# Masked attention in a six-layer decoder: the two terms of the scores issued term by term for a group of heads instead of head by head

## The chip, the cores and the metric

The kernel runs on one core of one Trainium2 chip. The metric is the device time of one execution in microseconds (us); for the kernel before it is the median of three runs. A core has TensorE (PE in the profile; PEld is its weight load), VectorE (DVE), ScalarE (ACT), GpSimd (POOL) and SyncE (SP), which issues the transfers.

## The reference, cut to what matters

Two stacks of layers follow one another on a sequence of 256 tokens of width 1024: four layers (windowed attention, a gated linear recurrence, MLA attention, windowed attention again, each with a cross attention to a memory and a gated feed-forward part), then two layers (attention with forget gates, here called fox, and dilated attention, each with memory heads and a feed-forward part). All is computed in float32. In two of them a score is the sum of two terms. The MLA layer has eight heads, and a causal mask:

```
sc = (einsum('bqhd,bkhd->bhqk', qn_b, k_nope)
      + einsum('bqhd,bkd->bhqk', qr_b, k_rope)) * scale
sc = where(key_pos[None, :] <= q_pos[:, None], sc, NEG)
p = softmax(sc)
```

Here `qn_b` and `k_nope` have 128 features for a head, the rotated parts `qr_b` and `k_rope` 64, and `k_rope` is shared by the heads. The fox layer has twelve heads of 64 features, and `c` is the running sum of the logarithm of the forget gates:

```
sc = einsum('bhqd,bhkd->bhqk', qi, k) * scale
sc = sc + ci[..., :, None] - c[..., None, :]
sc = where(kpos[None, :] <= qpos[:, None], sc, NEG_2)
p = softmax(sc)
```

Every other attention (windowed, dilated, cross and memory heads) has a single feature product in its score.

## The kernel before, in words

The tokens lie in two tiles of 128 (t = 0 and 1). Projections are built from `mm3` (L87 to L89): both factors are split into a rounded part and a rest in the format fp32r, and three products are accumulated. A weight is loaded by SyncE, rounded by ScalarE (`hi`, L76) and its rest taken by VectorE (`lo`, L81).

All attentions go through `attend` (called from `cross`, `swa`, `mla` and `mix`), once for each query tile, with 128 or 256 keys for tile 0 and 1 where the attention is causal. It works through groups of heads (eight heads at 128 keys, four at 256) in three steps: `scores` makes the scores of a group in two PSUM banks and their softmax, `turn` transposes the probabilities on TensorE (L334), `values` multiplies them by the values (L354). Scores of one group are issued ahead of the turn and the values of earlier ones. Heads alternate between the two banks: even heads go to bank 0, odd heads to bank 1.

Where a mask is given, `pre` writes it into both banks first, by products with a unit matrix (L291); fox adds the first half of the gate term there. Then `score(h)` gives the terms of head h, a list of pairs of a stationary and a moving operand, which are accumulated onto the open bank (L300). Without `pre` (cross attention and memory heads) each head is an accumulation of its own (L298). What `score` returns:

- `mla`: two terms, `(qT, kT)` of 128 rows in plain float32 (in the profile `xh,qT`, as the keys lie in the buffer `xh`), and `(qT, krT)` of 64 rows in plain float32, rows 0 to 63 for even and 64 to 127 for odd heads;
- fox (`mix(0)`): two terms, `(sel, cT)` of 128 rows in fp32r (in the profile `cT,sel`), and `(qT, kT)` of 64 rows in plain float32 (`kv,qT`), again the lower rows for even and the upper for odd heads;
- windowed (`swa`) and dilated (`mix(1)`) attention: one term of 64 rows in the same manner.

After the scores, VectorE takes the row maxima (L308), ScalarE the exponentials with their sums (L315), VectorE scales them (L321, L324); copies out of PSUM alternate between the two (`evac`, L62 and L64). In `mla` the query blocks of the last head groups are rotated on VectorE (L262 to L265), transposed (L161) and copied out (L64) just ahead of the first scores.

The order on each engine is not that of the source alone: a scheduler of the framework places instructions of neighbouring steps among one another, so that a few `mm3` of the next projection stand between parts of an attention. Each engine then executes its own instructions in that order and waits for the others by semaphores.

Of the kernel before, what the change touches and what calls it, by code (L numbers as in the profile page):

```python
# [34 lines left out]
def model_kernel(ctx: ExitStack, tc: tile.TileContext, A, out):  # L35
    nc = tc.nc
    V, S, G, T = nc.vector, nc.scalar, nc.gpsimd, nc.tensor
# [9 lines left out]
    def bank(tag="r"):  # L47
        return psum.tile([P, 512], F32, tag=tag, name="bank", bufs=4 if tag == "r" else 2)

    def bank_of(t):  # L50
        return bank(f"t{t}")
# [7 lines left out]
    def evac(dst, src):  # L59
        count["ev"] += 1  # L60
        if count["ev"] % 2:
            S.copy(dst, src)  # L62
        else:
            V.tensor_copy(dst, src)  # L64
# [26 lines left out]
    def split(hi, lo, src):  # L91
        S.copy(hi, src)  # L92
        V.tensor_tensor(lo, src, hi, ALU.subtract)

    def tile_cols(t):
        return slice(t * P, (t + 1) * P)
# [182 lines left out]
    def attend(ph, t, heads, d, keys, score, value, scale=1.0, pre=None, sinks=None, base=0, pb=2, tb=4):  # L279
        nk = keys // P  # L280
        size = 2 * (512 // keys)
        oth, otl = cur["o"]

        def scores(h0):
            n = min(size, heads - h0)
            g = n // 2
            banks = [bank()[:, : g * keys].rearrange("p (h n) -> p h n", n=keys) for _ in range(2)]
            if pre is not None:
                for b in range(2):
                    for j, (l, r) in enumerate(pre(slice(h0 + b, h0 + n, 2), g)):  # L290
                        T.matmul(banks[b], l, r, start=(j == 0), stop=False)  # L291
            for i in range(g):
                for b in range(2):
                    terms = score(h0 + 2 * i + b)
                    for j, (l, r) in enumerate(terms):
                        last = j == len(terms) - 1
                        if pre is None:
                            T.matmul(banks[b][:, i], l, r, start=(j == 0), stop=last)  # L298
                        else:
                            T.matmul(banks[b][:, i], l, r, start=False, stop=(last and i == g - 1))  # L300
            nm = sm.tile([P, 8], F32, tag="nm", name="nm")
            den = sm.tile([P, 8], F32, tag="den", name="den")
            pr = ph.tile([P, 2, 512], F32, tag="pr", name="pr", bufs=pb)
            prv = pr[:, :, : g * keys].rearrange("p b (h n) -> p b h n", n=keys)
            rd = sm.tile([P, 8], F32, tag="rd", name="rd")
            for b in range(2):
                c = slice(b * g, b * g + g)
                V.tensor_reduce(nm[:, c], banks[b], AX.X, ALU.max, negate=True)  # L308
                if sinks is not None:
                    V.tensor_tensor(nm[:, c], nm[:, c], sinks[1][:, h0 + b : h0 + n : 2], ALU.min)  # L310
                if scale != 1.0:
                    V.tensor_scalar(nm[:, c], nm[:, c], scale, None, ALU.mult)
                for i in range(g):
                    j = slice(b * g + i, b * g + i + 1)
                    S.activation(prv[:, b, i], banks[b][:, i], AF.Exp, bias=nm[:, j], scale=scale, accum_out=den[:, j])  # L315
                if sinks is not None:
                    es = sm.tile([P, 4], F32, tag="es", name="es")
                    V.tensor_tensor(es[:, :g], nm[:, c], sinks[0][:, h0 + b : h0 + n : 2], ALU.add)
                    S.activation(es[:, :g], es[:, :g], AF.Exp)
                    V.tensor_tensor(den[:, c], den[:, c], es[:, :g], ALU.add)  # L320
                V.reciprocal(rd[:, c], den[:, c])  # L321
                for i in range(g):
                    j = slice(b * g + i, b * g + i + 1)
                    V.tensor_scalar(prv[:, b, i], prv[:, b, i], rd[:, j], None, ALU.mult)  # L324
            return h0, n, prv

        def turn(h0, n, prv):
            pT = {}
            items = [(h, kt) for b in range(2) for h in range(b, n, 2) for kt in range(nk)]
            for o in range(0, len(items), 4):  # L330
                part = items[o : o + 4]
                tp = bank_of(t)
                for j, (h, kt) in enumerate(part):
                    T.transpose(tp[:, tile_cols(j)], prv[:, h % 2, h // 2, tile_cols(kt)], ident)  # L334
                dst = ph.tile([P, 4, P], F32, tag="pT", name="pT", bufs=tb)
                m = len(part)
                evac(dst[:, :m], tp[:, : m * P].rearrange("p (h n) -> p h n", n=P))
                for j, it in enumerate(part):
                    pT[it] = dst[:, j]
            return h0, n, pT  # L340

        def values(h0, n, pT):
            per = max(1, P // d)
            cols = n * d // P
            for c0 in range(0, cols, 4):
                nc_ = min(4, cols - c0)
                po = bank_of(t)
                for c in range(c0, c0 + nc_):
                    for i in range(per):
                        h = (c * P) // d + i  # L350
                        w = min(d, P)
                        off = (c * P) % d if d > P else 0
                        for kt in range(nk):
                            T.matmul(  # L354
                                po[i * w : (i + 1) * w, tile_cols(c - c0)],
                                value(h0 + h, kt)[:, off : off + w],
                                pT[h, kt],
                                start=(kt == 0),
                                stop=(kt == nk - 1),
                            )  # L360
                b0 = base + h0 * d // P + c0
                view = po[:, : nc_ * P].rearrange("p (b n) -> p b n", n=P)
                split(oth[:, b0 : b0 + nc_, tile_cols(t)], otl[:, b0 : b0 + nc_, tile_cols(t)], view)

        todo = list(range(0, heads, size))
        made, turned = [], []
        for i in range(len(todo) + 2):
            if i < len(todo):
                made.append(scores(todo[i]))
            if i >= 2:  # L370
                values(*turned.pop(0))
            if 1 <= i <= len(todo):
                turned.append(turn(*made.pop(0)))
# [415 lines left out]
    def load_norms(l):  # L789
        gb = par.tile([P, 2, D], F32, tag="gb", name="gb", bufs=1)  # L790
        nc.sync.dma_start(gb, A["norms"][l].partition_broadcast(P))
        return gb
# [169 lines left out]
    for i in range(4):  # L962
        kind, j = i % 3, i // 3
# [10 lines left out]
    with phase("g") as ph:  # L974
        g = ph.tile([P, D], F32, tag="g", name="g", bufs=1)
# [6 lines left out]
    g = load_norms(0)  # L982
# [3 lines left out]
    g = load_norms(1)  # L986
# [129 lines left out]
```

## Time and profile before

| what | value |
|---|---|
| runs | 2142.24, 2142.79, 2148.39 us, median 2142.79 us |
| span of the profiled execution | 2141.0 us |
| TensorE busy | 2103.1 us, 98% |
| weight loads (PEld) busy | 1869.3 us, 87% |
| VectorE, ScalarE, GpSimd busy | 1616.3, 1219.2, 84.4 us |
| mean granted clock of TensorE | 0.987 of full speed |
| read from memory | 354.81 MB, 166 GB/s over the span |

The span goes from the first to the last instruction of one profiled execution. TensorE's matmuls are pipelined, so the durations of neighbours overlap and the pace is read from the difference of two start times. A plain float32 product leaves two records in the profile, an fp32r product one. The granted clock is a share of 2.4 GHz: 1.00 is the full 2.4 GHz, 0.50 is 1.2 GHz.

### The profile page before, as it was taken

The page shows a single profiled execution, that of the slowest core. Times are in us where ns is not written, and L with a number is a line of the kernel's source. Part 1 is how long each engine was busy: PE and PEld are TensorE (multiplying, and loading weights), DVE is VectorE, ACT ScalarE, POOL GpSimd, SP SyncE. Part 2 cuts the span into 40 slices and gives each one's busy share as a digit, 9 for nine tenths or more (in the row PEclk, how much of TensorE's full clock was granted, in tenths as well). Part 3 has the DMA queues.
Part 4 walks back from the last instruction along what each step waited for, and adds up shares of the span by engine and source line. Part 5 has one row for each costly group of instructions (what it writes and reads, how often), then busy time and mean ns, then how long its engine had stood idle before and what let it go on. Part 6 is the DMA issues. An engine that isn't in the chain of part 4 may idle for free.

```text
span 2141.0 us, 36194 instructions
## 1 busy us (share of the span) xinstructions
PE 2103.1 (98%) x13528; PEld 1869.3 (87%) x13528; DVE 1616.3 (75%) x3344; ACT 1219.2 (57%) x2654; POOL 84.4 (4%) x77
## 2 busy tenths in 40 slices
PE   8999999999999999999999999999999999999998
PEld 7778999887999986899997789998878999978997
DVE  6877877898777784787788778888458877677775
ACT  5545656585555563555555456564446566456664
POOL 0010000122000001000000100000000000000000
PEclk9999999999999997999999999999999999999999
DMA  8533655526455461556544347654325655524651
GB/s 329 179 109 125 222 186 187 180 93 230 160 196 185 129 208 40 177 187 193 182 159 148 118 147 247 197 178 156 136 79 187 215 181 166 188 92 158 201 184 60
DMA packets 101409, 358.23 MB, mean 167 GB/s; under 512 B 11888, under 2 KB 13552, under 8 KB 99312
## 3 DMA queue, kind: packets, MB, share of 16 engines
q1 hardware_dynamic: 101232, 355.91, 50.2%
q8 instruction: 106, 1.74, 0.3%
q14 instruction: 71, 0.58, 0.1%
HBM read 354.81 MB, written 1.05 MB: 166 GB/s over the span
## 4 chain that ended last, share of the span: by engine, by line
PE 90%; DVE 5%; ACT 2%; issue 1%; DMA 1%; POOL 1%; SPq 0%; POOLq 0%; DVEq 0%; ACTq 0%
PE bank L87 26%; PE bank L88 26%; PE bank L89 26%; PE bank L354 3%; PE bank L161 3%; PE bank L300 3%; PE bank L334 2%; PE bank L298 1%; DVE lo L81 1%; ACT hi L76 1%; PE bank L291 1%; PE bank L768 0%; DMA row<-in_mem 0%; ACT pr L315 0%; DMA stage<-in_memT 0%
## 5 line engine op out<-in xcount | busy, mean ns | idle before, releaser
L76 ACT CAST hi<-raw 128x512 fp32r<-128x512 f32 (+3 forms) x1300 | 746.2, 606 | 480.9 <-PE bank L89 221.8
L81 DVE TENSOR_TENSOR lo<-raw,hi 128x512 fp32r<-128x512 f32 (+3 forms) x1289 | 840.6, 674 | 180.1 <-ACT hi L76 175.5
L87 PE MATMUL bank<-xh,hi 128*128 128x256 f32 x1920 | 543.6, 283 | 0.0
L89 PE MATMUL bank<-xh,lo 128*128 128x256 f32 x1920 | 543.2, 283 | 0.0
L88 PE MATMUL bank<-xl,hi 128*128 128x256 f32 x1920 | 543.2, 283 | 0.0
L87 PEld LDWEIGHTS bank<-xh,hi 128*128 128x128 f32 x1920 | 368.5, 192 | 3.3 <-issue 0.2
L88 PEld LDWEIGHTS bank<-xl,hi 128*128 128x128 f32 x1920 | 368.2, 192 | 2.8
L89 PEld LDWEIGHTS bank<-xh,lo 128*128 128x128 f32 x1920 | 368.2, 192 | 0.5
L87 PE MATMUL bank<-hi,xh 128*128 128x256 f32 (+4 forms) x784 | 263.4, 336 | 0.2
L722 DVE SCALAR_TENSOR_TENSOR c<-bank,cw,c 128x254 f32<-128x254 f32 (+1 forms) x528 | 238.9, 477 | 31.9 <-ACT c L718 31.5
L89 PE MATMUL bank<-hi,xl 128*128 128x256 f32 (+4 forms) x784 | 262.0, 335 | 0.0
L88 PE MATMUL bank<-lo,xh 128*128 128x256 f32 (+4 forms) x784 | 260.6, 333 | 0.0
L87 PE MATMUL bank<-hi,gh 128*128 128x512 f32 x528 | 207.9, 394 | 0.3 <-ACT gh L92 0.2
L88 PE MATMUL bank<-lo,gh 128*128 128x512 f32 x528 | 206.9, 392 | 0.0
L89 PE MATMUL bank<-hi,gl 128*128 128x512 f32 x528 | 205.4, 390 | 0.0
L87 PEld LDWEIGHTS bank<-hi,xh 128*128 128x128 f32 x784 | 149.0, 190 | 11.9 <-ACT row L62 1.4
L89 PEld LDWEIGHTS bank<-hi,xl 128*128 128x128 f32 x784 | 148.9, 190 | 9.9 <-issue 0.8
L88 PEld LDWEIGHTS bank<-lo,xh 128*128 128x128 f32 x784 | 148.9, 190 | 9.5 <-issue 0.5
L88 PE MATMUL bank<-lo,oh 128*128 128x512 f32 (+1 forms) x392 | 154.3, 394 | 2.0 <-POOL lo L81 1.0
L87 PE MATMUL bank<-hi,oh 128*128 128x512 f32 (+1 forms) x392 | 154.8, 398 | 0.0
L89 PE MATMUL bank<-hi,ol 128*128 128x512 f32 (+1 forms) x392 | 152.8, 391 | 0.0
L718 ACT ACTIVATE c<-bank,cw 128x256 f32<-128x256 f32 x264 | 133.5, 559 | 0.2 <-PE bank L89 0.2
(270 smaller groups left out, 2629.6 us busy)
## 6 DMA issues: line engine op xcount, KB each, us to landing
raw<-in_f_w_up SPq DMA_DIRECT2D x176, 512.0 KB, 4.3
raw<-in_f_w_down SPq DMA_DIRECT2D x88, 512.0 KB, 3.8
raw<-in_m_w_up SPq DMA_DIRECT2D x88, 512.0 KB, 4.2
raw<-in_m_w_down SPq DMA_DIRECT2D x44, 512.0 KB, 3.8
raw<-in_m_w_qkv SPq DMA_DIRECT2D x48, 384.0 KB, 3.8
raw<-in_x_w_q SPq DMA_DIRECT2D x32, 512.0 KB, 3.5
raw<-in_x_w_o SPq DMA_DIRECT2D x32, 512.0 KB, 4.8
gb<-in_ln_gb SPq DMA_DIRECT2D x12, 1024.0 KB, 4.8
```

What stands on the lines that cost most here:

```text
L76: S.copy(hi[:, c], raw[:, c])
L81: eng.tensor_tensor(lo[:, c], raw[:, c], hi[:, c], ALU.subtract)
L87: T.matmul(ps, ah, bh, start=first, stop=False)
L88: T.matmul(ps, ah, bl, start=False, stop=False)
L89: T.matmul(ps, al, bh, start=False, stop=last)
L161: T.transpose(ps[:w, j * P : (j + 1) * P], b, ident)
L291: T.matmul(banks[b], l, r, start=(j == 0), stop=False)
L300: T.matmul(banks[b][:, i], l, r, start=False, stop=(last and i == g - 1))
L334: T.transpose(tp[:, tile_cols(j)], prv[:, h % 2, h // 2, tile_cols(kt)], ident)
L354: T.matmul(po[i * w : (i + 1) * w, tile_cols(c - c0)], value(h0 + h, kt)[:, off : off + w], pT[h, kt], start=(kt == 0), stop=(kt == nk - 1),)
L718: S.activation(c[:, h], ps[:, h], AF.Identity, scale=cw[:, 2, b : b + 1], bias=cw[:, 3, b : b + 1])
L722: V.scalar_tensor_tensor(c[:, h, s:], ps[:, h, : 256 - s], cw[:, 2 - s, b : b + 1], c[:, h, s:], ALU.mult, ALU.add)
```

## The change

In `scores`, the terms of all heads of a group are collected first. Where there is no `pre`, the loops run as before. Where there is one, the loop over the terms is now the outer one: the first term of every head of the group, then the second term of every head. The head that closes the accumulation (`stop`) is still the last of each bank. For an attention with a single term the order stays what it was. The code grows by one line, so that lines below it move by one (L300 is L301, L334 is L335).

```
-            for i in range(g):
-                for b in range(2):
-                    terms = score(h0 + 2 * i + b)
-                    for j, (l, r) in enumerate(terms):
-                        last = j == len(terms) - 1
-                        if pre is None:
-                            T.matmul(banks[b][:, i], l, r, start=(j == 0), stop=last)
-                        else:
-                            T.matmul(banks[b][:, i], l, r, start=False, stop=(last and i == g - 1))
+            terms = {(i, b): score(h0 + 2 * i + b) for i in range(g) for b in range(2)}
+            if pre is None:
+                for (i, b), pairs in terms.items():
+                    for j, (l, r) in enumerate(pairs):
+                        T.matmul(banks[b][:, i], l, r, start=(j == 0), stop=(j == len(pairs) - 1))
+            else:
+                count_ = len(terms[0, 0])
+                for j in range(count_):
+                    for (i, b), pairs in terms.items():
+                        T.matmul(banks[b][:, i], *pairs[j], start=False, stop=(j == count_ - 1 and i == g - 1))
```

TensorE in the MLA layer, at the scores of query tile 0, before (`qn` and `qr` are blocks of queries that are still being transposed, the last `qr` of tile 0 for heads 6 and 7):

```order
L161 MATMUL bank<-ident,qn 128x128 x2
L291 MATMUL bank<-maskh,identr 128x512
L300 MATMUL bank<-xh,qT 128x128
L300 MATMUL bank<-krT,qT 128x128
L300 MATMUL bank<-xh,qT 128x128
L161 MATMUL bank<-ident,qr 128x128
L300 MATMUL bank<-krT,qT 128x128
L300 MATMUL bank<-xh,qT 128x128
L300 MATMUL bank<-krT,qT 128x128
L291 MATMUL bank<-maskh,identr 128x512
L300 MATMUL bank<-xh,qT 128x128
L300 MATMUL bank<-krT,qT 128x128
```

And the same place now, up to the end of tile 0:

```order
L161 MATMUL bank<-ident,qn 128x128 x2
L291 MATMUL bank<-maskh,identr 128x512
L301 MATMUL bank<-xh,qT 128x128 x3
L161 MATMUL bank<-ident,qr 128x128
L291 MATMUL bank<-maskh,identr 128x512
L301 MATMUL bank<-xh,qT 128x128 x3
L161 MATMUL bank<-ident,qr 128x128
L301 MATMUL bank<-xh,qT 128x128 x2
L301 MATMUL bank<-krT,qT 128x128 x5
L161 MATMUL bank<-ident,qr 128x128
L301 MATMUL bank<-krT,qT 128x128 x3
```

The eight first terms now stand together, and of the eight rope terms the last three stand behind the transposition of one more rotated block, which is that of tile 1's last group and stood behind tile 0's scores before.

VectorE at the end of the same place, before, with the row maxima L308 of tile 0:

```order
L81 TENSOR_TENSOR lo<-raw,hi 128x512
L265 TENSOR_TENSOR qr<-qr,rt 128x128
L308 TENSOR_REDUCE nm<-bank 128x4
L64 COPY qT<-bank 128x384
L312 TENSOR_SCALAR nm<-nm 128x4
L308 TENSOR_REDUCE nm<-bank 128x4
```

And now:

```order
L81 TENSOR_TENSOR lo<-raw,hi 128x512
L265 TENSOR_TENSOR qr<-qr,rt 128x128
L81 TENSOR_TENSOR lo<-raw,hi 128x512
L64 COPY qT<-bank 128x384
L309 TENSOR_REDUCE nm<-bank 128x4 x2
L313 TENSOR_SCALAR nm<-nm 128x4
```

One weight split (L81) and the copy of the rotated block now stand ahead of both row maxima.

TensorE in the fox layer, at the first group of query tile 0, before:

```order
L291 MATMUL bank<-sel,cT 128x512
L291 MATMUL bank<-maskh,identr 128x512
L300 MATMUL bank<-cT,sel 128x128
L300 MATMUL bank<-kv,qT 128x128
L300 MATMUL bank<-cT,sel 128x128
L300 MATMUL bank<-kv,qT 128x128
```

And now:

```order
L291 MATMUL bank<-sel,cT 128x512
L291 MATMUL bank<-maskh,identr 128x512
L301 MATMUL bank<-cT,sel 128x128 x8
L301 MATMUL bank<-kv,qT 128x128 x8
```

What alternated eight times is now one run of eight and another run of eight; the other groups of the layer change in the same way.

## Rows read from the trace of the kernel before

**Rows 1.** The page: span, TensorE's clock in 40 slices, the ending chain by engine.
```profile
span 2141.0 us, 36194 instructions
...
PEclk9999999999999997999999999999999999999999
...
PE 90%; DVE 5%; ACT 2%; issue 1%; DMA 1%; POOL 1%; SPq 0%; POOLq 0%; DVEq 0%; ACTq 0%
```

**Rows 2.** Stretches: length, busy PE, PEld, DVE, ACT, POOL, granted clock, DMA share, GB/s.
```profile
808.00:810.00 2.00, 1.65 (x6) 1.21 (x6) 1.84 (x7) 0.00 (x0) 0.00 (x0) 0.65 0.00 0
...
832.00:834.00 2.00, 2.00 (x10) 1.22 (x9) 1.18 (x2) 0.59 (x1) 0.00 (x0) 0.88 0.00 0
...
1162.00:1164.00 2.00, 1.32 (x12) 1.05 (x12) 1.42 (x7) 1.62 (x3) 0.00 (x0) 0.50 0.00 0
...
1538.00:1542.00 4.00, 4.00 (x19) 2.88 (x18) 0.54 (x1) 0.00 (x0) 0.00 (x0) 1.00 0.00 0
...
1542.00:1544.00 2.00, 2.00 (x9) 1.58 (x8) 1.00 (x3) 1.81 (x11) 0.00 (x0) 0.61 0.00 0
...
1556.00:1558.00 2.00, 2.00 (x20) 1.74 (x20) 2.00 (x6) 1.34 (x3) 0.00 (x0) 0.98 0.00 0
...
1880.00:1884.00 4.00, 4.00 (x38) 3.62 (x38) 3.19 (x8) 3.14 (x14) 0.00 (x0) 1.00 0.78 252
...
1890.00:1898.00 8.00, 6.92 (x57) 5.11 (x58) 6.36 (x18) 7.71 (x20) 0.00 (x0) 1.00 0.22 67
```

**Rows 3.** TensorE in time order, MLA attention: start, us, engine, line, operation, out<-in, records.
```profile
805.28 0.48 PE L300 MATMUL bank<-krT,qT 64*128 64x128 f32 x2
805.70 0.49 PE L300 MATMUL bank<-xh,qT 128*128 128x128 f32 x2
...
833.36 0.70 PE L300 MATMUL bank<-xh,qT 128*128 128x256 f32 x2
833.99 0.70 PE L300 MATMUL bank<-krT,qT 64*128 64x256 f32 x2
...
836.97 1.50 PE L354 MATMUL bank<-pT,xl 128*128 128x128 f32 x12
838.31 0.60 PE L334 MATMUL bank<-ident,pr 128*128 128x128 f32 x4
```

**Rows 4.** TensorE in time order, fox attention, tile 0 and tile 1.
```profile
1537.33 0.33 PE L300 MATMUL bank<-cT,sel 128*128 128x128 f32 x1
1537.59 0.48 PE L300 MATMUL bank<-kv,qT 64*128 64x128 f32 x2
1538.00 0.33 PE L300 MATMUL bank<-cT,sel 128*128 128x128 f32 x1
...
1571.22 0.38 PE L300 MATMUL bank<-cT,sel 128*128 128x256 f32 x1
...
1572.16 0.39 PE L300 MATMUL bank<-cT,sel 128*128 128x256 f32 x1
```

**Rows 5.** TensorE in time order, dilated attention, tile 0 and tile 1.
```profile
1879.95 1.16 PE L300 MATMUL bank<-kv,qT 64*128 64x128 f32 x16
1881.05 0.39 PE L291 MATMUL bank<-dh,identr 128*128 128x256 f32 x1
...
1881.38 0.28 PE L291 MATMUL bank<-dh,identr 128*128 128x256 f32 x1
1881.50 0.28 PE L291 MATMUL bank<-dl,identr 128*128 128x256 f32 x1
...
1903.66 1.13 PE L300 MATMUL bank<-kv,qT 64*128 64x256 f32 x8
1904.72 0.50 PE L291 MATMUL bank<-dh,identr 128*128 128x512 f32 x1
```

**Rows 6.** VectorE and ScalarE in time order, MLA attention.
```profile
805.03 0.28 DVE L265 TENSOR_TENSOR qr<-qr,rt 128x128 f32<-128x128 f32 x1
...
813.66 1.28 ACT L315 ACT_TABLE_LOAD   x1 [10.54 <-DVE nm L312]
```

## The prediction, made before the changed kernel ran

> **What bounds the kernel now.** I read the page first, then the granted clock in stretches of 2 us, then TensorE's instructions in order of time in the two stages that the change touches, and last the same in a third stage that already has the order the change makes. The page says that TensorE is the bound: 90% of the chain that ended last lies on it [rows 1]. A stage gets shorter only if TensorE gets through it sooner. The row of the clock shows one clearly weak slice, 0.7 of full speed [rows 1]. In stretches of 2 us there are two long falls to 0.50, that is to 1.2 GHz: 1.4 us of the stretch 808 to 810 are low and 0.5 us of 832 to 834, so the first lasts from 808.6 to 832.5, 23.9 us; the second, by the same reading, from 1542.4 to 1556.1, 13.6 us [rows 2]. The first is the attention of the MLA layer (function mla), the second that of the forget-gate layer (mix(0), below called fox). Those are the only two callers with a `pre` and two score terms, so the only ones whose order changes.
>
> In both stages TensorE counts as busy and yet moves slowly. In MLA one record of a 128-column term takes 0.21 us (0.42 for two, from 805.28 to 805.70) and one of 256 columns 0.315 us (0.63 for two) [rows 3]. In fox one head, which is one record of the first term and two of the second, takes 0.67 us at 128 columns and 0.94 us at 256 [rows 4]. A product of plain fp32 leaves two records (x2), the fp32r first term of fox one (x1) [rows 3, 4]. Now the comparison. The dilated layer runs the same second term (kv,qT, 64 rows of the array, neighbours on opposite halves) with nothing between: 16 records from 1879.95 to 1881.05, 0.069 us each, and at 256 columns 8 records in 1.06 us, 0.1325 each [rows 5]. And plain fp32 records of 128 rows that follow one another, the value products in MLA, take 1.34 us for 12, 0.112 each [rows 3]. So 0.1 us or more is lost at each change between a term of 128 rows and one of 64, and the halves of the array don't work side by side. The alternation costs the time, not the products.
>
> **The change part by part.** No instruction is added or removed; products move. In MLA the first terms (xh,qT) of the heads of a group stand together, then the rope terms (krT,qT); in fox the fp32r terms (cT,sel), then kv,qT. I take 0.2 us for each change of kind that remains, from the 0.42 us that two records take now against 0.22 unmixed [rows 3].
>
> MLA, query tile 0, 128 columns: now 32 records by 0.21 = 6.7 us. After: 16 by 0.112 = 1.8, 16 by 0.069 = 1.1, three changes 0.6, together 3.5. Gain 3.2 us.
> MLA, tile 1, 256 columns: now 32 by 0.315 = 10.1 us. After: 16 by 0.224 = 3.6 (twice the 128-column price), 16 by 0.1325 = 2.1, four changes 0.8, together 6.5. Gain 3.6 us.
> Fox, tile 0: now 12 heads by 0.67 = 8.0 us. After: 12 first terms by 0.12 = 1.4, 24 records by 0.069 = 1.7, two changes 0.4, together 3.5. Gain 4.5 us.
> Fox, tile 1: now 12 by 0.94 = 11.3 us. After: 1.4, 24 by 0.1325 = 3.2, three changes 0.6, together 5.2. Gain 6.1 us.
> These are prices at full clock. Sum: 17.4 us.
>
> Two prices have no row of their own. Successive fp32 terms of 128 rows and 256 columns: between 0.224 and today's 0.315; I take the low end, as the two rows of 64-row products scale with columns in the same way (0.069 to 0.1325); the high end costs 16 by 0.09 = 1.5 us. Successive cT,sel: the nearest row is the mask's fp32r product of 256 columns, 0.12 us (1881.38 to 1881.50) [rows 5]; it may be less at 128 columns (0.06, worth 0.7 us), and at most the 0.26 that it takes now (1537.33 to 1537.59) [rows 4], which costs 24 by 0.14 = 3.4 us.
>
> The Trainium skill, TensorEngine Tiling (Array Packing), section Theoretical Speedup, gives products with 64 rows or fewer up to twice the pace. The rows show three times (0.41 us for two in fox [rows 4] against 0.069 each [rows 5]), since the change of kind goes as well; that page's Key Properties say that changing the tiling mode drains TensorE. By a factor of two on the 64-row records alone the 17.4 us would be 10 to 11; I go by the rows.
>
> **The clock.** Work done at 1.2 GHz takes twice its time. 23.9 + 13.6 = 37.5 us at half clock hold 18.8 us that full clock gives back. In fox the clock fell after TensorE had been busy without a gap (4.00 of 4.00 us from 1538 to 1542, clock 1.00) [rows 2]: what stood there was the alternation of kinds, nothing else. The dilated layer's same stretch, without alternation, stays at 1.00 (1880 to 1884) [rows 2]. I therefore take the fall as following from the alternation, and it goes with it. 17.4 + 18.8 = 36.2 us if TensorE never had to wait.
>
> **New waits.** It will. MLA first: the rotated queries of the last head group come late. VectorE ends that rotation at 805.3 (L265 at 805.03, 0.28) [rows 6]; in the new order TensorE has its six first terms done near 804.0 and waits 1.1 us to transpose, then 1.0 us for VectorE to split one weight piece and copy the block out. The last three krT terms of tile 0 now stand behind the transposition of tile 1's last rotated block, and on VectorE one more weight split (L81) and the copy of that block stand ahead of the tile's row maxima. That is a new dependence, but tile 0 is still complete near 808.1, and ScalarE, which now loads its table for this tile at 813.66 [rows 6], does so at 810.2 by my count. From there the exponentials set the pace: TensorE waits about 0.9 us for the first scaled probabilities, 0.7 for the second half, 0.7 for their copies out, and about 1 us in the last group. Rounded, 5 us of waits in MLA. Fox has the pieces ready, and mm3 products (L87 to L89) stand between; the probabilities that the first transposes wait for come at about 1541.5 by my count, when TensorE is just through the second group. I take 1.2 us for each tile, 2.4 together. 36.2 - 7.4 = 28.8 us. Waits of this kind can lower the clock elsewhere: in the fourth layer's windowed attention it is at 0.50 with TensorE busy 1.32 of 2 us [rows 2]. For one such fall, which I put at 5.6 us, under half of the shorter of the two present ones, I take off its half, 2.8. That leaves **26.0 us**. Behind the two stages follow the output projections, with TensorE busy and weights split ahead; they start earlier and lose nothing. VectorE's weight splits, SyncE's weight loads and GpSimd keep their order except the few named.
>
> The profiled execution spans 2141.0 us [rows 1], 1.8 us under the median of the runs, 2142.8. I take the difference off the median: 2142.8 - 26.0 = 2116.8.
>
> **Rivals.**
> First, the clock falls all the same. The order makes TensorE quick and then idle. The row of the windowed attention speaks for it; against it speaks the dilated layer, which has the order that the change makes and such waits too (TensorE busy 6.92 of 8 us from 1890 to 1898), at 1.00 [rows 2]. Then the 18.8 us stay lost, the 17.4 are kept, and a slower TensorE waits less, some 3.5 us: 14 us, 2129. In its favour stands also the Trainium skill, TensorE: Matmul & The Clock Gate, section HAM oscillation: waits of TensorE bring the half clock. The trace agrees at 1162 and shows at 1542 a fall without a wait, so the rule alone doesn't account for the case; by it alone 2129 would be the time.
> Second, no measurable change: the 64-row products don't run side by side when they accumulate onto an open bank, and the softmax chain on VectorE and ScalarE takes the rest. Then only the changes of kind go, and 3 us are left: 2140. Against it: the dilated layer's products also accumulate onto a mask written before.
> Third, slower: with bursts and waits the clock stays low through both attentions whole, 41 us in MLA (801.8 to 842.4) and 62 us in fox (1536 to 1598), 103 us in place of 37.5. That is 33 us more against 14 won: 2161. It begins to cost when more than 37.5 + 2 by 14 = 66 us lie at half clock. Nothing in the trace has a fall that long, and dense value products end the present one at 832.5.
> That the change does nothing can be left out: the order of instructions shows it at every group of both layers.
>
> **How the numbers follow.** Forecast 0.74, clock still falling 0.19, no change 0.05, slower 0.02. About 0.3%, 6.4 us, is what a measurement of this kernel can tell from no change. Forecast and first rival are both faster by more: 0.93; same 0.05; slower 0.02. The range goes from 2109, where the fp32r terms are cheap and most waits don't show, to 2131, which takes in the first rival and the high ends of both unknown prices.
>
> **What would show it.** In the changed profile: kv,qT of fox tile 0 as one run of 16 records near 1.1 us; successive xh,qT at 0.11 us (128 columns) and 0.22 (256); the stretch of MLA from the first mask product to the last value product about 26 us long instead of 41, fox tile 0 about 10 us shorter, tile 1 about 5; granted clock 1.00 in fox's tile 0 and no 24 us fall in MLA; in their place waits of TensorE for VectorE's copies and scaled probabilities. I am wrong if runs of 64-row products keep 0.2 us a record, if half clock spans as much as before, or if TensorE's waits in MLA are well above 5 us.

## The result, and the profile after

The changed kernel takes 2111.65 us (median of 4 runs, 2111.48 to 2114.15); the kernel before, run beside it, 2142.69. The ratio is 0.9857, with a 95% interval of 0.9839 to 0.9875: 31.0 us faster. The prediction was 2116.8 us in a range of 2109 to 2131.

The page of the changed kernel, as in [rows 1], with the row of busy times:

```profile
span 2112.4 us, 36195 instructions
...
PE 2071.3 (98%) x13528; PEld 1853.0 (88%) x13528; DVE 1613.5 (76%) x3344; ACT 1218.4 (58%) x2654; POOL 84.3 (4%) x77
...
PEclk9999999999999999999999999999999999999999
...
PE 89%; DVE 5%; ACT 3%; issue 1%; POOL 1%; DMA 1%; POOLq 0%; DVEq 0%; SPq 0%; ACTq 0%
```

TensorE is the bound as before, and has the same 13,528 matmuls, but is busy 31.8 us less (2103.1 before). The weak slice of the clock, 0.7 in [rows 1], is gone.

Next the three stretches that the change touches, each from about its first to its last product on TensorE: MLA, fox tile 0, fox tile 1. The columns are length, busy PE, PEld, DVE, ACT, POOL, granted clock, DMA share, GB/s. First the kernel before:

```profile
801.50:842.40 40.90, 40.12 (x155) 27.09 (x156) 20.64 (x59) 13.02 (x43) 0.00 (x0) 0.71 0.16 56
1536.00:1569.60 33.60, 33.58 (x169) 25.23 (x168) 18.71 (x47) 18.46 (x56) 0.00 (x0) 0.80 0.22 74
1569.60:1598.00 28.40, 28.40 (x164) 18.57 (x163) 17.54 (x44) 12.51 (x43) 0.00 (x0) 1.00 0.19 62
```

The same three in the changed kernel, and a piece of its MLA stage:

```profile
802.50:831.70 29.20, 27.23 (x158) 21.47 (x159) 20.16 (x59) 12.99 (x42) 0.00 (x0) 0.88 0.21 76
1521.99:1545.80 23.81, 23.17 (x170) 19.21 (x169) 17.74 (x47) 17.94 (x56) 0.00 (x0) 1.00 0.28 93
1545.80:1568.90 23.10, 22.38 (x168) 16.34 (x166) 17.12 (x44) 12.48 (x43) 0.00 (x0) 1.00 0.26 87
...
808.00:810.00 2.00, 2.00 (x13) 1.55 (x13) 0.96 (x3) 0.00 (x0) 0.00 (x0) 0.50 0.56 190
```

Three things are in these lines. The stages are 11.7, 9.8 and 5.3 us shorter, 26.8 of the 28.6 us between the two spans. The clock went from 0.80 to 1.00 in fox tile 0, but only from 0.71 to 0.88 in MLA: 6.8 us of that stage lie at 0.50 in this execution. And TensorE, which was idle 0.8 us in the three stages together (0.78, 0.02, 0.00), is now idle 3.3 us (1.97, 0.64, 0.72).

TensorE in time order shows the runs that the change makes (start, us, engine, line, operation, out<-in, records, idle before and its releaser). Fox tile 0, then MLA:

```profile
1523.11 1.00 PE L301 MATMUL bank<-cT,sel 128*128 128x128 f32 x8
1524.04 1.16 PE L301 MATMUL bank<-kv,qT 64*128 64x128 f32 x16
1525.14 0.38 PE L291 MATMUL bank<-sel,cT 128*128 128x256 f32 x1
...
1526.18 0.72 PE L301 MATMUL bank<-kv,qT 64*128 64x128 f32 x8
```

```profile
804.59 0.50 PE L291 MATMUL bank<-maskh,identr 128*128 128x512 f32 x1 [0.65 <-DVE qT L64]
...
806.92 0.83 PE L301 MATMUL bank<-xh,qT 128*128 128x128 f32 x4 [0.74 <-DVE qT L64]
...
817.74 0.52 PE L335 MATMUL bank<-ident,pr 128*128 128x128 f32 x2 [0.48 <-DVE pr L325]
```

Eight heads of fox take 0.93 (1523.11 to 1524.04) and 1.10 us (1524.04 to 1525.14), 2.03 in place of 8 by 0.67 = 5.4 [rows 4]. In MLA the three waits are the ones that were foreseen, for VectorE's copies and scaled probabilities; they are short. One such wait was there before the change, just ahead of the fall of the clock at 808.6:

```profile
808.35 0.60 PE L300 MATMUL bank<-xh,qT 128*128 128x128 f32 x2 [0.65 <-DVE qT L64]
```

### The profile page after: what moved, and what is told of

It is laid out like the page before. It is cut to its first block, busy times and chain, and to the rows that moved or that the text cites. A ratio compares the mean times of both kernels' runs of the same rounds, so it can differ in the third digit from the quotient of the medians.

```text
span 2112.4 us, 36195 instructions
## 1 busy us (share of the span) xinstructions
PE 2071.3 (98%) x13528; PEld 1853.0 (88%) x13528; DVE 1613.5 (76%) x3344; ACT 1218.4 (58%) x2654; POOL 84.3 (4%) x77
## 4 chain that ended last, share of the span: by engine, by line
PE 89%; DVE 5%; ACT 3%; issue 1%; POOL 1%; DMA 1%; POOLq 0%; DVEq 0%; SPq 0%; ACTq 0%
PE bank L87 26%; PE bank L88 26%; PE bank L89 26%; PE bank L355 3%; PE bank L161 3%; DVE lo L81 2%; PE bank L335 2%; PE bank L301 1%; PE bank L296 1%; ACT pr L316 1%; ACT hi L76 1%; PE bank L291 1%; DMA row<-in_mem 0%; PE bank L769 0%; DVE nm L309 0%
## 5 line engine op out<-in xcount | busy, mean ns | idle before, releaser
L81 DVE TENSOR_TENSOR lo<-raw,hi 128x512 fp32r<-128x512 f32 (+3 forms) x1289 | 840.2, 673 | 182.3 <-ACT hi L76 177.6
L89 PEld LDWEIGHTS bank<-hi,xl 128*128 128x128 f32 x784 | 148.7, 190 | 10.2 <-issue 1.0
```

Source lines behind the costliest of these rows:

```text
L81: eng.tensor_tensor(lo[:, c], raw[:, c], hi[:, c], ALU.subtract)
L89: T.matmul(ps, al, bh, start=False, stop=last)
```

## Experiments

The stretches at half clock differ between executions of one kernel, so a measure without them helps below. The table shows what they cost. MLA in the old order takes 40.86, 39.40 and 37.76 us with 23.9, 20.5 and 17.1 us at 0.50, and fox tile 1 takes 28.48 and 42.27 with none and 30.7: about 0.45 us of length for each us at 0.50. The *time at full clock* is here the span less 0.45 us for each us at 0.50. Without a profile the time at 0.50 follows from the mean granted clock: it is twice the share by which that lies under 1, times the span.

Over 29 executions of the kernel before, whose times were 2132.5 to 2150.2 us, the time at full clock stayed between 2115.8 and 2120.5, 2118.5 in the mean. For the changed kernel (12 executions, 2108.8 to 2118.4 us) it is 2104.8. So of the 30 us between the means of the spans some 14 are work that TensorE no longer does, and 16 are clock. The price is not exact: over the executions of one kernel the span grows by 0.41 us for each us at 0.50 (0.41 also for the changed kernel, 0.42 for the variant with MLA alone), which would make it 15 and 15. Stage lengths in the profiled executions (us; "low" is the time at 0.50 in that stage, and the last column is the mean over all executions of a kernel):

| kernel | MLA | low | fox tile 0 | low | fox tile 1 | low | at full clock, whole |
|---|---|---|---|---|---|---|---|
| before | 40.86 | 23.9 | 33.62 | 13.6 | 28.48 | 0 | 2118.5 |
| before, second and third profile | 39.40, 39.40 | 20.5, 20.5 | 33.60, 33.60 | 13.7, 13.7 | 28.48, 28.48 | 0, 0 | |
| changed | 29.16 | 6.8 | 23.80 | 0 | 23.15 | 0 | 2104.8 |
| changed, second and third profile | 26.07, 26.05 | 0, 0 | 23.81, 23.79 | 0, 0 | 23.14, 23.15 | 0, 0 | |
| only MLA | 29.17 | 6.8 | 35.07 | 17.1 | 42.27 | 30.7 | 2113.7 |
| only fox | 37.76 | 17.1 | 23.81 | 0 | 23.14 | 0 | 2108.7 |
| head by head, first term on 64 rows | 37.74 | 17.1 | 26.86 | 6.8 | 23.91 | 0 | 2109.9 |
| second term by half | 31.46 | 10.2 | 24.11 | 0 | 24.26 | 0 | 2107.8 |
| by pair | 28.79 | 0 | 24.83 | 0 | 23.44 | 0 | 2108.2 |
| changed, MLA in groups of four | 26.68 | 0 | 23.80 | 0 | 23.14 | 0 | 2106.1 |
| changed, first term on 64 rows | 26.06 | 0 | 23.42 | 0 | 23.15 | 0 | 2104.5 |

### Each half of the change alone

In the changed kernel a switch chooses the order, set for `mla` alone or for fox alone; nothing else differs.

```
-                for j in range(count_):
-                    for (i, b), pairs in terms.items():
+                steps = [(j, k) for k in terms for j in range(count_)]
+                if by_term:
+                    steps.sort(key=lambda s: s[0])
+                for j, (i, b) in steps:
```

The changed kernel itself was run along with them.

> The changed kernel once more, unaltered, to see which falls of TensorE's clock belong to the change and which come and go. Theory: 2111 to 2115 us; a fall of 5 to 7 us in the MLA attention behind the waits for the rotated queries again, none in the fox attention; falls elsewhere (windowed attention, recurrence) may sit in other places than in the first profile. Rival, that the 31 us are all in the two attentions: these two stages would then be shorter by 31 us together; the first profile shows 26.8 (MLA 11.7, fox tile 0 9.8, tile 1 5.3).

> Term by term in the MLA layer alone, fox head by head as before. Theory (each stage pays for its own alternation): MLA shorter by 11 to 13 us, the fox stage keeps 0.67 us a head and its fall of the clock near the end of tile 0's first group; time 2143 - 12 = 2129 to 2132. Rival (one fall of the clock brings on the next): the fall in fox disappears as well, fox tile 0 shorter by 6 us, 2124.

> Term by term in the fox layer alone, MLA head by head as before. Theory: fox shorter by 15 us, the MLA layer keeps its long half-clock stretch of some 24 us; time 2126 to 2128. With the run of MLA alone the gains add up to 26 to 31 us. Rival (the gains aren't independent): the sum of both gains is under 22 us or over 34.

Measured: the changed kernel 2113.74 us, ratio 0.9861 (0.9838 to 0.9884); MLA alone 2134.71, 0.9974 (0.995 to 0.9997); fox alone 2124.81, 0.9917 (0.9898 to 0.9937). By time the gains are 7.0 and 16.9 us, 23.9 together, under the 26 to 31 that were expected; the whole change gained 27.9 beside them. MLA alone missed its range of 2129 to 2132, and fox alone came out a little under its 2126 to 2128. At full clock MLA gives 4.8 us and fox 9.8; together they make 14.6, against 13.7 for the whole change, so the two parts add up nearly. What doesn't add up is the clock. With MLA alone it fell further in fox than before, in two pieces (columns as above):

```profile
1530.00:1546.00 16.00, 16.00 (x51) 11.09 (x52) 8.50 (x30) 8.02 (x34) 0.00 (x0) 0.52 0.00 1
...
1564.00:1592.00 28.00, 28.00 (x91) 17.08 (x90) 10.06 (x27) 7.40 (x28) 0.00 (x0) 0.50 0.04 14
```

17.1 and 30.7 us at 0.50 where the kernel before had 13.6: that takes back all of MLA's gain in this execution, one of the slowest of ten (2144.9 us; they scatter widely, 2126.5 to 2145.2). With fox alone MLA still falls, for 17.1 us, and fox does not. So the fall in fox does not follow from the one in MLA: it goes with fox's own order.

The repeat showed something else than expected. The same program as in the first profile has no fall in MLA this time (TensorE in time order, then two stretches):

```profile
806.60 0.71 PE L301 MATMUL bank<-xh,qT 128*128 128x128 f32 x4 [0.74 <-DVE qT L64]
...
809.58 1.89 PE L301 MATMUL bank<-xh,qT 128*128 128x256 f32 x8
811.40 1.14 PE L301 MATMUL bank<-krT,qT 64*128 64x256 f32 x8
```

```profile
806.00:808.00 2.00, 1.40 (x14) 1.26 (x14) 2.00 (x8) 0.00 (x0) 0.00 (x0) 1.00 0.80 258
...
1160.00:1162.00 2.00, 2.00 (x10) 1.02 (x6) 0.84 (x2) 1.18 (x4) 0.00 (x0) 0.50 0.32 84
```

The wait of 0.74 us is there as before, and the clock stays at 1.00; MLA then takes 26.07 us. The fall is in the windowed attention of the fourth layer instead, 17.1 us. A wait of 1.53 us stands just ahead of it; the same wait stands there in the other two profiles of the changed kernel without a fall, and in the three of the kernel before with one of 6.8 us.

### Is it the change between 128 and 64 rows?

Taken from the kernel before, so head by head. The gate term of fox needs few rows; its weights are put into both halves of the array, so that each head's first term runs on 64 rows, on the same half as its second term (the lines that copy the rows of `c` to the upper half are not shown). Data types and the alternation of an fp32r and a plain product stay.

```
-                        terms.insert(0, (sel[:, 0, h : h + 1].to_broadcast([P, P]), cT[:, :n]))
+                        terms.insert(0, (sel[r, 0, h : h + 1].to_broadcast([64, P]), cT[r, :n]))
...
-    sel = np.stack([one, -one], 1)
+    both = ((q % 64 == h) | (q % 64 == h + 32)).astype(f)
+    sel = np.stack([both, -one], 1)
```

> Head by head everywhere, as before, but the first term of fox takes 64 rows in place of 128, the same half of the array as the head's second term (its 24 rows of data are copied to the upper half for the odd heads; the result is the same). So the order alternates as before, fp32r and plain fp32 too, but the array's division into halves doesn't change. Theory (changing between 128 and 64 rows costs, and keeps the halves from working side by side): a head of fox tile 0 takes 0.2 to 0.3 us in place of 0.67, no fall of the clock in fox, the gain is that of fox alone, 13 to 15 us: 2128. Rival (changing between fp32r and fp32, or between the weights of two terms, costs): a head keeps 0.55 to 0.67 us and the clock falls, 2141 to 2144. MLA is as before in both.

Measured: 2128.18 us, ratio 0.993 (0.9907 to 0.9952). TensorE in time order in fox, eight heads:

```profile
1533.09 0.33 PE L300 MATMUL bank<-cT,sel 64*128 64x128 f32 x2
1533.26 0.44 PE L300 MATMUL bank<-kv,qT 64*128 64x128 f32 x4
...
1534.63 0.38 PE L291 MATMUL bank<-sel,cT 128*128 128x256 f32 x1
...
1537.01 0.70 PE L298 MATMUL bank<-kmT,qT 64*128 64x256 f32 x2 [0.78 <-ACT pr L315]
```

Eight heads take 1.54 us (1533.09 to 1534.63), 0.19 for a head where the kernel before needs 0.67 [rows 4] and the changed one 0.25 (2.03 by 8). The order is the old one, and the loss is gone: in fox it sits in the change between a product of 128 rows and one of 64, not in the alternation of terms, of data types or of weights. The Trainium skill, TensorEngine Tiling (Array Packing), section Key Properties, says that a change of tiling mode drains TensorE. The trace agrees in that the change costs time, and puts a price on it below.

No fall had been expected in fox. The clock still fell in tile 0, for 6.8 us, after the wait of 0.78 us in the last line, which the kernel before doesn't have:

```profile
1540.00:1544.00 4.00, 4.00 (x13) 2.53 (x12) 2.66 (x10) 1.53 (x7) 0.00 (x0) 0.50 0.00 0
```

### Are the halves side by side only when neighbours alternate?

In the changed kernel the second term goes first over all heads of the lower half, then over all of the upper.

```
-                    for (i, b), pairs in terms.items():
+                    for (i, b), pairs in sorted(terms.items(), key=lambda kv: kv[0][::-1] if j else kv[0]):
```

> Term by term as in the changed kernel, but the second terms of all even heads stand together and then those of all odd heads, so that neighbours use the same half of the array and the same bank. Theory (a part of the gain is that neighbours work on opposite halves at once): a record of kv,qT takes 0.11 us at 128 columns in place of 0.069 and about 0.22 at 256 in place of 0.1325; 24 by 0.04 and 24 by 0.09 in fox, 16 and 16 in MLA, 5 us more than the changed kernel at full clock. Rival (only the number of changes between 128 and 64 rows counts): the records keep 0.069 and 0.1325 and the time is that of the changed kernel.

Measured: 2117.25 us, beside 2146.81 for the kernel before, ratio 0.9861 (0.984 to 0.9881). Fox, tile 0 and tile 1:

```profile
1528.71 1.71 PE L301 MATMUL bank<-kv,qT 64*128 64x128 f32 x16
1530.35 0.38 PE L291 MATMUL bank<-sel,cT 128*128 128x256 f32 x1
...
1531.39 0.72 PE L301 MATMUL bank<-kv,qT 64*128 64x128 f32 x8
...
1552.44 1.14 PE L301 MATMUL bank<-kv,qT 64*128 64x256 f32 x8
1553.51 0.48 PE L291 MATMUL bank<-sel,cT 128*128 128x512 f32 x1
```

At 128 columns 16 records take 1.64 us in place of 1.10, 0.10 each: sorted by half they lose part of the overlap. At 256 columns 8 records take 1.07, as many as the 1.06 of alternating halves [rows 5]. I had expected 0.22 each there, and that was wrong: with four records on the lower half ahead of four on the upper, the halves still ran side by side. It is the number of records that counts and not the columns: the group of four heads at 128 columns, also four records and four, takes 0.72 us here (1531.39) and 0.72 alternating (1526.18 in the changed kernel). The single records of the trace show how. Of the eight and eight, the upper half's first starts at 1529.26, right behind the fifth of the lower half, and its last five run alone; of the four and four, it starts 0.01 us after the lower half's first. Neighbours on opposite halves are not needed; a long enough run on one half costs. At full clock the whole kernel takes 3 us more than the changed one, where 5 were expected.

### How many changes must go?

Two heads at a time, first the first terms of an even and an odd head, then their second terms: half as many changes as before.

```
+                for i in range(g):
+                    for j in range(count_):
+                        for b in range(2):
+                            T.matmul(banks[b][:, i], *terms[i, b][j], ...)
```

> Half a dose: the first terms of two heads, then the second terms of the same two heads, so half as many changes between 128 and 64 rows as head by head, and both halves of the array in use. Theory: a pair of heads in fox costs two first terms by 0.12, four records by 0.069 and two changes by 0.16, 0.84 us or 0.42 a head (0.67 before, 0.25 in the changed kernel); 256 columns 0.55 a head (0.94 and 0.41). Over both layers 6 us more than the changed kernel at full clock, and the clock may fall in fox. Rival (the cost is per kind of term and not per change): as the changed kernel, 0.25 a head.

Measured: 2116.63 us, ratio 0.9861 (0.9843 to 0.9878). Fox, tile 0 and tile 1:

```profile
1525.05 0.44 PE L302 MATMUL bank<-cT,sel 128*128 128x128 f32 x2
1525.42 0.49 PE L302 MATMUL bank<-kv,qT 64*128 64x128 f32 x4
1525.84 0.44 PE L302 MATMUL bank<-cT,sel 128*128 128x128 f32 x2
...
1549.51 0.70 PE L302 MATMUL bank<-kv,qT 64*128 64x256 f32 x4
1550.15 0.50 PE L302 MATMUL bank<-cT,sel 128*128 128x256 f32 x2
```

A pair takes 0.79 us (1525.05 to 1525.84), 0.40 for a head: of the 0.42 us that a head saves by terms (0.67 to 0.25) the pair already saves 0.27. At full clock the kernel takes 3.4 us more than the changed one, where 6 were expected. The price of a burst follows from these runs. Of plain 64-row products at 256 columns, two records take 0.62 us (MLA, below), four 0.64, eight 1.06; at 128 columns four take 0.42, sixteen 1.10. Each further set of four costs 0.42 at 256 columns and about 0.22 at 128, and every burst some 0.2 us on top (from two lengths at either width). Two records cost what four cost, which fits a lone head leaving the other half empty.

MLA turned out to be a test of another kind. There the framework's scheduler put the mask of the second bank behind most heads of the first, so that the stage stayed head by head but for the last pair of each group. Yet its clock held:

```profile
809.23 0.50 PE L291 MATMUL bank<-maskh,identr 128*128 128x512 f32 x1
809.56 0.59 PE L302 MATMUL bank<-xh,qT 128*128 128x256 f32 x2
809.99 0.27 PE L161 MATMUL bank<-ident,qr 128*128 128x128 f32 x1
...
812.41 0.59 PE L302 MATMUL bank<-xh,qT 128*128 128x256 f32 x2
812.93 0.70 PE L302 MATMUL bank<-krT,qT 64*128 64x256 f32 x2
813.56 0.70 PE L302 MATMUL bank<-xh,qT 128*128 128x256 f32 x2
814.19 0.70 PE L302 MATMUL bank<-krT,qT 64*128 64x256 f32 x2
814.81 0.50 PE L291 MATMUL bank<-maskh,identr 128*128 128x512 f32 x1
```

The products of 128 rows pay at a change as well. A first term (xh,qT) takes 0.43 us between a mask and a transposition, both of 128 rows (809.56 to 809.99), 0.52 between a mask and a rope term (812.41 to 812.93), and 0.63 between two rope terms (813.56 to 814.19): some 0.1 us for each neighbour of 64 rows, ahead or behind.

The clock in the same stage:

```profile
808.00:816.00 8.00, 7.84 (x32) 4.49 (x32) 6.36 (x20) 4.64 (x19) 0.00 (x0) 1.00 0.30 89
816.00:832.00 16.00, 16.00 (x105) 12.96 (x104) 10.49 (x32) 8.27 (x24) 0.36 (x1) 1.00 0.07 24
```

This is the MLA stage in nearly its old order at full clock: 28.79 us. Term by term at full clock it takes 26.07, 2.7 us less; the kernel before would take 30.1 by the price of half clock above, so that the order itself is worth some 4 us there. The rest of the 11.7 to 14.8 us that MLA became shorter is clock. Nor is it luck of one execution: by their mean clocks the four runs by pair lie at 0.50 for 14.8 us in the whole kernel, as the changed kernel does (15.5), and those with MLA wholly in its old order and fox in the new one for 34.0.

### Can the waits in MLA, or what is left of the changes, be taken away?

Two variants of the changed kernel: groups of four heads in MLA also in tile 0, so that the softmax starts earlier; and the 64-row gate term of above together with the new order.

```
-        size = 2 * (512 // keys)
+        size = size or 2 * (512 // keys)
...
+                    scale=scale, pre=causal[t], size=4,
```

> The changed kernel, with groups of four heads instead of eight in query tile 0 of the MLA attention, so that the first group needs no block of queries that is still being rotated and its softmax starts earlier; two mask products of 256 columns more in place of one of 512 for each bank. Theory (the MLA stage is set by waits for the late blocks, and the fall of the clock follows these waits): the stage takes 23 to 25 us in place of 26.1 without a fall and 29.2 with one, and no fall in it; 2108 to 2112. Rival (the softmax chain sets the stage anyway): 26 to 29 us, as the changed kernel.

> The changed kernel, and in fox the first term with 64 rows on the head's own half of the array. Theory: two first terms side by side, 0.06 to 0.08 us each in place of 0.12, and one change less in each group, 1 to 2 us off the fox stage (23.8 and 23.1 us for the two tiles now, by then 23 and 22.5), as VectorE and ScalarE are close behind; 2110 to 2113. Rival (the chain behind the scores is the bound): no change.

Measured: four heads 2118.91 us, ratio 0.9869 (0.9849 to 0.9889); the 64-row gate term 2115.23, 0.9857 (0.9835 to 0.988). Both lie outside what was expected (2108 to 2112, and 2110 to 2113), and neither is distinguishable from the changed kernel. With four heads the waits for the copied query blocks only moved (0.65 us at 807.14, 0.72 at 809.60); MLA takes 26.68 us, without a fall, where 23 to 25 were expected and 26 to 29 were the rival's. With the 64-row gate term the first terms of eight heads take 0.50 us in place of 0.93:

```profile
1530.11 0.66 PE L301 MATMUL bank<-cT,sel 64*128 64x128 f32 x8
1530.61 1.10 PE L301 MATMUL bank<-kv,qT 64*128 64x128 f32 x16
...
1534.03 1.13 PE L296 MATMUL bank<-kmT,qT 64*128 64x256 f32 x4 [0.79 <-ACT pr L316]
```

Fox tile 0 is 0.4 us shorter by it (23.42), tile 1 is not (23.15): there TensorE's idle time grew from 0.72 to 1.14 us, so that the waits took what the products gave. Once the changes are down to two in a group, making the rest cheaper is worth little. The last line is the wait behind which the head-by-head variant with 64-row first terms fell to half clock; here it is as long, and fox stays at 1.00.

### Does the fall belong to the order, or to the execution?

The kernel before twice more and the changed kernel once more, none of them altered.

> The kernel before, unaltered, for a second profile of its falls of the clock. Theory (head by head, the two attentions draw long falls, of a length that differs from run to run): between 10 and 50 us at half clock in MLA and fox together, and a stage of MLA of 35 to 42 us, fox tile 0 of 31 to 36. Rival (the falls of the first profile were chance): under 8 us in the two together; MLA 29 us, as in the run by pairs, where MLA kept the order of the kernel before.

> The same a third time, with the same expectations: theory 10 to 50 us at half clock in MLA and fox together, rival under 8.

> The changed kernel a third time, with more runs for the ratio. Theory: 0 to 11 us at half clock in MLA (stage 26 or 29 us), none in fox (23.8 and 23.1 us); 2110 to 2116, span times mean clock 2102 to 2105. Rival (falls in fox come back in some executions): fox tile 0 above 26 us.

Measured: 2141.78 and 2142.19 us (one execution each), and 2114.61 (0.9862, 0.9844 to 0.988). The stage lengths are in the table, within what was expected; the span times the mean clock of the changed kernel, expected between 2102 and 2105, is 2104.9 in the mean of four. Stretches of the kernel before in its third profile, MLA and fox:

```profile
810.00:830.00 20.00, 20.00 (x51) 11.62 (x50) 8.63 (x29) 6.72 (x26) 0.00 (x0) 0.52 0.16 53
...
1542.00:1552.00 10.00, 10.00 (x28) 6.21 (x29) 4.52 (x19) 4.25 (x21) 0.00 (x0) 0.50 0.00 0
```

And of the changed kernel at the same places:

```profile
808.00:816.00 8.00, 7.30 (x41) 5.17 (x40) 6.28 (x23) 5.19 (x22) 0.00 (x0) 1.00 0.42 139
...
1518.00:1542.00 24.00, 23.36 (x170) 19.28 (x169) 17.59 (x46) 17.72 (x56) 0.00 (x0) 1.00 0.29 86
```

Count over all profiles. Fox head by head with 128-row first terms fell in four of four (13.6 or 13.7 us three times, 47.8 with MLA alone); fox term by term in none of seven, nor by pair, with half the changes, in its one profile; head by head with 64-row first terms it fell for 6.8 us. MLA head by head fell for 17.1 to 23.9 us in five of five, but not in the by-pair kernel, whose MLA is nearly the same order; term by term it fell for 6.8, 6.8 and 10.2 us in three of seven and not at all in four. In fox the long fall goes with the alternation of 128 and 64 rows; how the alternation brings it is not shown. In MLA the new order makes it shorter and rarer, and what decides in a single execution is not settled: the waits are the same with a fall and without.

## Why the prediction was right, and where its steps were off

**What bounds, and the cause.** Right. TensorE's time went down by 31.8 us, and the loss lay where the prediction put it, at the change between 128 and 64 rows; in fox the first term on 64 rows showed that with the old order kept, and in MLA the prices by neighbour in the by-pair profile.

**The records after.** kv,qT of fox tile 0 is one run of 16 records in 1.10 us (predicted near 1.1). Successive first terms of MLA at 256 columns take 1.82 us for 8 (809.58 to 811.40), 0.228 each (predicted 0.22, the low end of the two bounds). Successive cT,sel take 0.116 each (0.93 by 8; predicted 0.12). All score terms of MLA together take 10.1 us in the last profile of the changed kernel: its four kinds, each burst from its start to the next one's less waits, are 2.23, 1.50, 3.55 and 2.82. Predicted were 3.5 + 6.5 = 10.0.

**The gain at full clock.** Predicted were 17.4 us of products less 7.4 of waits, 10.0 in all. With 0.45 us for each us at 0.50 the stages go from 30.1 to 26.1 in MLA, from 27.5 to 23.8 in fox tile 0 and from 28.48 to 23.15 in tile 1: 4.0, 3.7 and 5.3 us, 13.0 together, and the means of all runs give 14. Set beside the idle time (0.65, 0.02 and 0 us before; 2.19, 0.64 and 0.71 in the repeat of the changed kernel), that splits as follows.

| stage | products: predicted | measured | new waits: predicted | measured | sum: predicted | measured |
|---|---|---|---|---|---|---|
| MLA | 6.8 | 5.5 | 5.0 | 1.5 | 1.8 | 4.0 |
| fox tile 0 | 4.5 | 4.3 | 1.2 | 0.6 | 3.3 | 3.7 |
| fox tile 1 | 6.1 | 6.0 | 1.2 | 0.7 | 4.9 | 5.3 |

(The measured products are the sum plus the added idle time.) The terms for fox are right. In MLA two were mis-sized, and they cancel in part. The term "32 by 0.21" and "32 by 0.315" charged every record as if the products on both sides of it were of the other kind. But in the old order many first terms have masks, transposes or value products beside them, which are of 128 rows as well, and each such neighbour makes a first term 0.1 us cheaper. The old order's score terms sum to 15.7 us at full clock (6.4 in tile 0, which lies ahead of the fall in the third profile of the kernel before, and 9.3 in tile 1 by the prices of the by-pair profile), where I had 16.8; less the 10.1 above that is 5.6, beside the 5.5 of the table. And the waits in MLA were more than three times too dear. Of the 2.1 us that I put down for the rotated queries and their copy, the kernel before already waited 0.65 (808.35); now it is 0.65 and 0.74. I had let TensorE wait for the exponentials of each group in turn; in the trace mm3 products and the next group's terms fill most of that, and one such wait is left: 0.48 us for scaled probabilities (817.74) in the first profile, 0.70 for exponentials in the two others.

**The clock.** Predicted were 18.8 us given back less 2.8 for a fall elsewhere, 16.0; measured are 16.4, from 51.9 to 15.5 us at 0.50 in the mean, by 0.45 each. The sum is right, but by two errors that cancel. "Work done at 1.2 GHz takes twice its time" was too much: by 0.45 it takes 1.8 times, and 37.5 us at half clock hold 17 us and not 18.8; the two later profiles have 34.1 there, 15 us. And the reserve of 2.8 for a new fall elsewhere was hardly needed. Outside the two stages the three profiles of each kernel have 14 us at half clock before and 13 now, in the mean, in other places from one execution to the next (12 to 18, and 5 to 24); inside them a fall of 6.8 us is left in one of three. The prediction was 5 us too slow: some 4 come from the work at full clock, where waits too dear outweigh products too dear, and 1 from medians against means.

**The reason for the clock.** "I take the fall as following from the alternation, and it goes with it" holds in fox for the long falls, all against none. For MLA it was too simple: by pair most of the alternation stands and the clock holds, and the changed kernel falls for 6.8 us in one execution and not in the next. The prediction also passed over the wait of 0.65 us just ahead of the fall in MLA before, and the idle time in its row at 1162 lies behind the start of that fall, which comes at 1160.2, at the end of a wait of 1.53 us. The Trainium skill, TensorE: Matmul & The Clock Gate, section HAM oscillation, has it that waits of TensorE bring half clock; its example has longer waits than any of these. The trace has falls behind waits: at 808 in MLA before (0.65 us) and in the changed kernel (0.65 and 0.74), at fox tile 0 of the 64-row variant (0.78), in the windowed attention (1.53). But fox before falls without one [rows 2], and all of these waits are found at 1.00 too: in the MLA of the by-pair kernel (0.65) and of the repeat (0.65 and 0.74), in fox tile 0 of the changed kernel with the 64-row gate term (0.79), in the windowed attention of the changed kernel (1.53). So waits of this size alone don't decide it, and what does stays open.

**The rivals.** The clock falling all the same (2129) would have shown half clock in fox, which is at 1.00 throughout. No change (2140) needed halves that don't work side by side on an open bank; 0.069 us a record refutes it. Slower (2161) needed 66 us or more at half clock; the falls inside the changed kernel's three profiles, all but the one at the very end, sum to 13.7, 20.5 and 3.4 us. The variant with MLA alone, with 47.8 us at half clock in fox in one execution, shows that such long falls do occur and can take back what a stage won.

## What to carry to other kernels

Look in TensorE's order of time for products of 64 rows between products of 128: a record that costs three times what it costs in a long run is the sign. Every burst of 64 rows costs some 0.2 us on top, and each neighbour of 128 rows some 0.1 us more, so collect those of one kind, or bring all to the same number of rows. When pricing a present order, price each record by what stands ahead of it and behind it, not by the dearest case. Look up which of the waits that a new order brings are there already. Compare variants by time at full clock as well as by time, and measure what half clock costs instead of taking it as half: over 29 executions of one kernel the first scattered by 5 us, the second by 18.

## What was not expected of the hardware

- Two plain 64-row records and four take the same time in a burst, 0.62 and 0.64 us at 256 columns: the second head is free, on the other half.
- The halves overlap even when four records of one half stand ahead of four of the other (1.07 us for eight at 256 columns, against 1.06 alternating; 0.72 at 128, in either order); with eight and eight at 128 columns part of it is lost (1.64 against 1.10), as the second half begins only behind the fifth record of the first.
- TensorE falls to half clock while busy without a gap (4.00 of 4.00 us from 1538 to 1542, [rows 2]), and whether it does can differ between executions of the same program, with the same waits, at the same place.
- A us at half clock cost these stages about 0.45 us of length, not 0.5: 28.48 us and 42.27 for the same products in fox tile 1, with none and 30.7 us at 0.50.
